# Forming three sums of input blocks from turned blocks alone, in the entries of a decoder block's three big products

## The chip, the cores and the metric

One core of one Trainium2 chip runs the whole kernel. The metric is the device time of one execution in microseconds (us), as the median of several runs.

## What is computed

A decoder block on 1024 tokens of width 1024 in float32: a SwiGLU half-step, a gated merge of two token mixers, a second half-step, a final norm. Cut to what matters here:

```python
h = x + 0.5 * swiglu(rms_norm(x, g1), w1, w3, w2)       # "f1"
proj = rms_norm(h, g2) @ w_in                           # "mix": q, k, v, pool input, gates
h = h + merged(proj) @ w_out
h = h + 0.5 * swiglu(rms_norm(h, g3), v1, v3, v2)       # "f2"
return rms_norm(h, g4)
```

Each of the three stages multiplies a normed input by wide weights: `rms_norm(h) @ w`.

## The kernel before

**Seven products.** The normed input is a matrix of 2 x 2 blocks: rows in two halves (token tiles 0 to 3, the lower, and 4 to 7, the upper; a tile is 128 tokens) and columns in two halves (LOWS, HIGHS, 512 each). As in Strassen's method in Winograd's form, a block product takes seven multiplications instead of eight. Their input sides are b11 and b21 (the lower tiles' two halves), b22 (the upper tiles' high half), and four sums: t1 = b12 - b11, t2 = b22 - t1, t3 = b22 - b12, t4 = t2 - b21, where b12 is the upper tiles' low half. All are held turned (features on the partitions), in two parts of a shorter format: `hi`, a rounded copy made by ScalarE, and `lo`, the remainder `source - hi`. A product is 12 matmuls of 128x512: weights hi by input hi, weights hi by input lo, weights lo by input hi.

**An entry.** `Entry.run` prepares the upper tiles while TensorE has products to do that need only b11 and b21. It occurs three times, in the stages f1, mix and f2. For each upper tile t: the norm scales the rows (`high(t, 1)`, VectorE, L282); TensorE turns b22 (`Rows`, four 128x128 transposes into one PSUM bank, L409), b12 (`turned`, four, L477) and the row difference HIGHS - LOWS, which POOL formed (L461; four transposes, L409). VectorE forms t1 in place of b12 (`first_less`, L471), t2 = turned difference + b11 (`second`, L465) and t4 in place of t2 (`fourth`, L468). The turned b11 and b21 of tile t - 4 are at hand in SBUF (`self.low`). `Parts` and `Rows` have ScalarE make the `hi` (L429, L411), and `lower` makes the `lo` on VectorE (L432, L416). Two products of TensorE stand in each turn of the loop, `product(i)` and `product(k)`; tile 7 has a passage of its own behind the loop, so that its first sums needed come first.

**Order.** The code runs under a manual schedule: each engine works through its instructions in the order in which the code issues them, and waits by semaphores for what another engine must have done. Two engines are kept from using one PSUM bank at a time: `second` therefore stands behind ScalarE's `hi` of the same bank. `self.more(n)` issues the operands of the first products behind the entry: the sum of weight blocks, ScalarE's rounding of it (L320, `wc`), and its remainder (L323, VectorE or POOL). The first of these products uses t2, then t3, t1 and t4 follow.

Of the kernel before, what the change touches and what calls it, by code (L numbers as in the profile page):

```python
# [10 lines left out]
F32 = mybir.dt.float32  # L11
F32R = mybir.dt.float32r
AF = mybir.ActivationFunctionType
OP = mybir.AluOpType
# [123 lines left out]
def tile_block(  # L138
# [29 lines left out]
    ve, ac, gp, pe = nc.vector, nc.scalar, nc.gpsimd, nc.tensor  # L168

    def sbuf(name, side="left", bufs=1):  # L170
        return tc.tile_pool(name=name, bufs=bufs, side=side, reuse_waits="tile")
# [7 lines left out]
    def bank(tag, name):  # L179
        return psum.tile([P, HALF], F32, tag=tag, name=name)  # L180
# [117 lines left out]
    LOWS, HIGHS = slice(0, HALF), slice(HALF, S)  # L298

    def sums_of_x(pool, name, order, **kw):  # L300
        return {
            s: tuple(pool.tile([P, 4, HALF], F32R, name=f"x{part}_{s}_{name}", **kw) for part in ("hi", "lo"))
            for s in order
        }
# [31 lines left out]
    class Quad:  # L336
# [49 lines left out]
        def run(self, m, back=True):  # L386
            if m not in self.w:
                self.operand(m)
            w, n = self.w.pop(m), self.n
            x = {1: "b11", 2: "b21", 3: "b22", 4: "t4", 5: "t1", 6: "t2", 7: "t3"}[m]  # L390
            key = {1: "x", 2: "x", 5: "v", 3: "v"}.get(m, m)
            first = key not in self.bank
            if first:
                self.bank[key] = bank("mm" if key in ("x", "v") else "acc", f"u_{self.sv.name}{n}{m}")
            self.sv.product(self.bank[key], w, x, start=first)
            if m == 3 and back:
                raws.back(2)
            return self.bank[key]

    class Rows:  # L400
# [14 lines left out]
        def lower(self):  # L415
            ve.tensor_tensor(self.lo, self.p, self.hi.bitcast(F32), op=OP.subtract)  # L416
# [5 lines left out]
    class Parts:  # L422
# [5 lines left out]
            self.src = src.rearrange("p (k q) -> p k q", k=4)  # L428
            ac.activation(self.hi, self.src, AF.Copy)  # L429

        def lower(self):
            ve.tensor_tensor(self.lo, self.src, self.hi.bitcast(F32), op=OP.subtract)  # L432

    class Entry:

# [17 lines left out]
        def run(self, high, after, first=0):  # L453


            X = self.sv.X

            def scaled_rows(t):
                y = high(t, 1)
                t3 = self.sv.half_tile("s", f"t3_{t}")  # L460
                gp.tensor_tensor(t3, y[:, HIGHS], y[:, LOWS], op=OP.subtract)  # L461
                return y, t3

            def second(r3, t2, t):
                ve.tensor_tensor(t2, r3.flat, self.low[t - 4][:, LOWS], op=OP.add)  # L465

            def fourth(t2, t):
                ve.tensor_tensor(t2, t2, self.low[t - 4][:, HIGHS], op=OP.subtract)  # L468

            def first_less(p12, t):  # L470
                ve.tensor_tensor(p12, p12, self.low[t - 4][:, LOWS], op=OP.subtract)  # L471

            def turned(y, t):
                p12 = bank("acc", f"x_b12_{t}")
                for j in range(4):
                    c = slice(j * P, (j + 1) * P)
                    pe.transpose(p12[:, c], y[:, c], ident)  # L477
                return p12

            y, t3 = scaled_rows(4)  # L480
            for t in range(4, NT - 1):
                i = first + 2 * (t - 4)
                k = i + 1
                self.product(i)
                self.operand(i + 2)
                high(t + 1, 0)
                s = Rows(X, "b22", y[:, HIGHS], t)
                self.out(i)
                p12 = turned(y, t)
                first_less(p12, t)  # L490
                r1 = Parts(X, "t1", p12, t)
                r3 = Rows(X, "t3", t3, t)
                t2 = bank("acc", f"x_t2_{t}")
                s.lower()
                r1.lower()
                self.product(k)
                y, t3 = scaled_rows(t + 1)
                self.operand(k + 2)
                second(r3, t2, t)
                r2 = Parts(X, "t2", t2, t)  # L500
                r3.lower()
                r2.lower()
                self.out(k)
                after(t)
                fourth(t2, t)
                if t < NT - 2:
                    r4 = Parts(X, "t4", t2, t)
                    if t > 4:
                        self.more(0, 1)
                    r4.lower()  # L510

            t = NT - 1
            i, k = i + 2, k + 2
            self.product(i)
            p3 = bank("acc", f"x_t3_{t}")
            p12 = turned(y, t)
            s = Rows(X, "b22", y[:, HIGHS], t, "mm")
            r3 = Rows(X, "t3", t3, t, p=p3)
            r4 = Parts(X, "t4", t2, t - 1)
            self.more(0, 2)  # L520
            t2 = bank("acc", f"x_t2_{t}")
            second(r3, t2, t)
            r4.lower()
            r2 = Parts(X, "t2", t2, t)
            r3.lower()
            self.more(0)
            r2.lower()
            self.product(k)
            self.out(i)
            first_less(p12, t)  # L530
            r1 = Parts(X, "t1", p12, t)
            self.more(1)
            r1.lower()
            fourth(t2, t)
            r4 = Parts(X, "t4", t2, t)
            s.lower()
            r4.lower()
            self.out(k)
            after(t)
# [366 lines left out]
    X = sums_of_x(scope.enter_context(sbuf("x1")), "f1", SUMS)  # L906
# [971 lines left out]
    def combine(hp, half, adds, lower):  # L1878

        c = (LOWS, HIGHS)[half]  # L1880
        o = [own[hp, g][:, c] for g in range(GROUPS)]
        for g in range(GROUPS):
            ve.tensor_tensor(o[g], o[g], factor_rows(hp, g, half), op=OP.mult)
            if g > 0:
                adds[g - 1].tensor_tensor(o[g], o[g], o[g - 1], op=OP.add)
            yield
        if half == 0:
            att_parts[hp] = [part_tile(f"att{hp}_{part}") for part in range(2)]
        hi, lo = (v[:, c] for v in att_parts[hp])
        ac.activation(hi, o[2], AF.Copy)  # L1890
        lower.tensor_tensor(lo, o[2], hi.bitcast(F32), op=OP.subtract)
        yield
# [114 lines left out]
    with tc.manual_schedule():  # L2007
# [3 lines left out]
        load_gate(1)  # L2011
        factors = [make_factors(hp, eng) for hp, eng in enumerate((gp, ve))]
        combines = [[combine(hp, half, adds, lower) for half in range(2)]
                    for hp, (adds, lower) in enumerate((((gp, gp), gp), ((gp, ve), ve)))]
        splits = {}
        for q in range(N // 2):
# [80 lines left out]
    op = wo.enter_context(sbuf("ops", "right"))  # L2097
# [390 lines left out]
```

## Time and profile before

| | |
|---|---|
| median of 3 runs | 1890.03 us (1889.73 to 1890.55) |
| span of the profiled execution | 1888.4 us |
| TensorE (PE) busy | 1878.1 us, 99% |
| VectorE (DVE) busy | 1345.8 us, 71% |
| ScalarE (ACT) busy | 773.1 us, 41% |
| POOL busy | 715.0 us, 38% |

The profiled execution is one run on the chip, and its times are those from which the terms below are taken. Its own time is not given apart from the span, which goes from its first to its last instruction. A row of the timeline reads: start in us from the start of the span, duration in us, engine, line of the kernel, operation, output<-input by the program's names (buffer numbers left out), shapes, the count of instructions merged into the row, and in brackets how long the engine sat idle before it and for whom. x_b is a PSUM bank with turned rows (b11, b12, b22), x_t one with a sum; xhi and xlo are the parts.

### The profile page before, as it was taken

What the parts mean: (1) busy time and instruction counts of PE and PEld (TensorE: products, weight loads), DVE (VectorE), ACT (ScalarE), POOL (GpSimd) and SP (SyncE); (2) the same over time, 40 slices, a digit from 0 to 9 for tenths busy, and PEclk for the clock granted to TensorE, in tenths of its full rate; (3) what the DMA queues carried; (4) which work ended last, traced back from release to release, by engine and by line L of the source; (5) the groups of instructions that cost most, each with busy time, mean ns of one, the idle gap of its engine ahead of it and who ended that gap; (6) DMA issues with size and microseconds to landing.
All of it is one profiled execution on the core that took longest, in us unless ns stands there. A gap on an engine that the chain in (4) does not pass through costs nothing.

```text
span 1888.4 us, 24712 instructions
## 1 busy us (share of the span) xinstructions
PE 1878.1 (99%) x8806; PEld 1559.8 (83%) x8806; DVE 1345.8 (71%) x1988; ACT 773.1 (41%) x1395; POOL 715.0 (38%) x536
## 2 busy tenths in 40 slices
PE   9999999999999999999999999999999999999998
PEld 8888888888888888888888888888888888888886
DVE  6877666558786776657885897887665566577867
ACT  7423333333344543334445772363233333334344
POOL 5433333331223354434555357543333333312221
PEclk9999999999999999999999999999999999999999
DMA  6154423336565526765578968644332223354654
GB/s 258 34 201 158 139 93 115 126 117 217 171 230 197 184 90 217 231 221 200 206 245 315 321 221 297 260 150 155 140 129 96 87 102 118 135 193 159 225 198 145
DMA packets 146035, 334.98 MB, mean 177 GB/s; under 512 B 17784, under 2 KB 39288, under 8 KB 144376
## 3 DMA queue, kind: packets, MB, share of 16 engines
q1 hardware_dynamic: 142168, 322.55, 49.4%
q10 hardware_dynamic: 3744, 10.85, 1.6%
q8 instruction: 69, 1.13, 0.2%
q14 instruction: 54, 0.44, 0.1%
HBM read 232.76 MB, written 100.60 MB: 177 GB/s over the span
## 4 chain that ended last, share of the span: by engine, by line
PE 54%; DVE 3%; ACT 2%; issue 1%; DMA 1%; POOL 0%; ACTq 0%; SPq 0%; DVEq 0%; POOLq 0%
PE u_mixm L332 15%; PE d_f L846 8%; PE wo L2168 4%; PE yp L1910 1%; PE u_f20b L332 1%; PE u_f21a L332 1%; PE u_f210b L332 1%; PE u_f210a L332 1%; PE u_f29b L332 1%; PE u_f29a L332 1%; PE u_f28b L332 1%; PE u_f28a L332 1%; PE u_f27b L332 1%; PE u_f27a L332 1%; PE u_f26b L332 1%; PE u_f25b L332 1%
## 5 line engine op out<-in xcount | busy, mean ns | idle before, releaser
L846 PE MATMUL d_f<-bhi_f,ahi_f 128*128 128x512 f32 x616 | 240.2, 390 | 0.0
L846 PE MATMUL d_f<-bhi_f,alo_f 128*128 128x512 f32 x616 | 239.7, 389 | 0.0
L846 PE MATMUL d_f<-blo_f,ahi_f 128*128 128x512 f32 x616 | 239.6, 389 | 0.0
L803 POOL TENSOR_TENSOR alo_f<-g_f,ahi_f 128x512 fp32r<-128x512 f32 x60 | 86.5, 1457 | 273.1 <-ACT ahi_f L799 273.1
L332 PE MATMUL u_mixm<-xhi_t_mix,wc_mixm 128*128 128x512 f32 x608 | 157.3, 391 | 0.2 <-ACT wc_mixm L320 0.2
L846 PEld LDWEIGHTS d_f<-bhi_f,ahi_f 128*128 128x128 f32 x616 | 115.6, 188 | 24.2 <-ACT h L420 0.4
L846 PEld LDWEIGHTS d_f<-bhi_f,alo_f 128*128 128x128 f32 x616 | 115.6, 188 | 24.1
L846 PEld LDWEIGHTS d_f<-blo_f,ahi_f 128*128 128x128 f32 x616 | 115.6, 188 | 23.9
L332 PEld LDWEIGHTS u_mixm<-xhi_t_mix,wc_mixm 128*128 128x128 f32 x608 | 113.5, 188 | 24.0 <-ACT wc_mixm L320 0.7
L332 PE MATMUL u_mixm<-xhi_b_mix,wc_mixm 128*128 128x512 f32 x456 | 120.3, 391 | 0.0
L323 POOL TENSOR_TENSOR wc_mixm<-s_mixm,wc_mixm 128x512 fp32r<-128x512 f32 x52 | 76.8, 1477 | 107.1 <-ACT wc_mixm L320 94.2
L332 PEld LDWEIGHTS u_mixm<-xhi_b_mix,wc_mixm 128*128 128x128 f32 x456 | 84.9, 188 | 17.3
L320 ACT ACTIVATE wc_mixm<-s_mixm 128x512 fp32r<-128x512 f32 x76 | 47.0, 628 | 111.8 <-DVE s_mixm L374 56.0
L799 ACT ACTIVATE ahi_f<-g_f 128x1024 fp32r<-128x1024 f32 x84 | 81.9, 975 | 4.9 <-DMA g_f<-gs_f 4.9
L332 PE MATMUL u_mixm<-xlo_t_mix,wc_mixm 128*128 128x512 f32 x304 | 81.3, 389 | 0.0
L323 POOL TENSOR_TENSOR wc_mixm<-raw,wc_mixm 128x512 fp32r<-128x512 f32 x40 | 60.2, 1505 | 40.2 <-ACT wc_mixm L320 29.5
L2168 PE MATMUL wo<-w_o,o_hi 128*128 128x512 f32 x224 | 69.4, 391 | 0.0
L799 ACT ACTIVATE bhi_f<-s_f2w 128x512 fp32r<-128x512 f32 x55 | 32.9, 628 | 86.3 <-DVE s_f2w L821 67.3
L799 ACT ACTIVATE bhi_f<-s_f1w 128x512 fp32r<-128x512 f32 x55 | 33.0, 629 | 83.6 <-DVE s_f1w L821 70.3
L332 PEld LDWEIGHTS u_mixm<-xlo_t_mix,wc_mixm 128*128 128x128 f32 x304 | 57.1, 188 | 12.0
L803 DVE TENSOR_TENSOR alo_f<-g_f,ahi_f 128x1024 fp32r<-128x1024 f32 (+1 forms) x48 | 57.6, 1200 | 9.4 <-ACT ahi_f L799 9.4
L332 PE MATMUL u_mixm<-xlo_b_mix,wc_mixm 128*128 128x512 f32 x228 | 61.0, 389 | 0.0
(1351 smaller groups left out, 4765.5 us busy)
## 6 DMA issues: line engine op xcount, KB each, us to landing
g_f<-gs_f SPq DMA_DIRECT2D x70, 512.0 KB
gs_f<-y_f SPq DMA_DIRECT2D x88, 256.0 KB
raw<-in_w2a_dram SPq DMA_DIRECT2D x35, 512.0 KB
raw<-in_w2b_dram SPq DMA_DIRECT2D x35, 512.0 KB
gs_f<-gb_f SPq DMA_DIRECT2D x46, 256.0 KB
raw<-in_w1a_dram SPq DMA_DIRECT2D x22, 512.0 KB
raw<-in_w3a_dram SPq DMA_DIRECT2D x22, 512.0 KB
raw<-in_w1b_dram SPq DMA_DIRECT2D x22, 512.0 KB
```

The source lines that it names most:

```text
L320: ac.activation(w[:, 0], src, AF.Copy)
L323: eng.tensor_tensor(w[:, 1], src, w[:, 0].bitcast(F32), op=OP.subtract)
L332: pe.matmul(p, a, b, start=(start and n == 0), stop=(n == 11), skip_group_check=not start)
L799: ac.activation(hi[:, c], src, AF.Copy)
L803: eng.tensor_tensor(lo[:, d], src[:, o], hi[:, d].bitcast(F32), op=OP.subtract)
L846: pe.matmul(self.banks[m][t], l, r, start=(first and q == 0), stop=(last and q == 2))
L1910: pe.matmul(p, a, b, start=(j == 0), stop=(j == 11))
L2168: pe.matmul(banks[m][t], l, r, start=(st == 0 and j == 0 and q == 0), stop=(st == 1 and j == 1 and q == 2))
```

## The change

The row difference, its POOL instruction and its four transposes are gone, so an upper tile takes eight transposes. t1 is written to an SBUF tile and no longer in place of b12, so the bank with b12 stays; t2 is formed as turned b22 - t1 (`second`), and t3 as t2 - b11 (`third`, written over the bank with b12). In tiles 4 to 6 the remainder of t1 is made by POOL instead of VectorE. `first_less` of tile 7 stands ahead of `second`, no longer near the end.

```diff
-        def lower(self):
-            ve.tensor_tensor(self.lo, self.src, self.hi.bitcast(F32), op=OP.subtract)
+        def lower(self, eng=ve):
+            eng.tensor_tensor(self.lo, self.src, self.hi.bitcast(F32), op=OP.subtract)
...
             def scaled_rows(t):
-                y = high(t, 1)
-                t3 = self.sv.half_tile("s", f"t3_{t}")
-                gp.tensor_tensor(t3, y[:, HIGHS], y[:, LOWS], op=OP.subtract)
-                return y, t3
-
-            def second(r3, t2, t):
-                ve.tensor_tensor(t2, r3.flat, self.low[t - 4][:, LOWS], op=OP.add)
+                return high(t, 1)
+
+            def first_less(p12, t):
+                t1 = self.sv.half_tile("s", f"t1_{t}")
+                ve.tensor_tensor(t1, p12, self.low[t - 4][:, LOWS], op=OP.subtract)
+                return t1
+
+            def second(s, t1, t2):
+                ve.tensor_tensor(t2, s.flat, t1, op=OP.subtract)
+
+            def third(t2, p, t):
+                ve.tensor_tensor(p, t2, self.low[t - 4][:, LOWS], op=OP.subtract)
...
-            def first_less(p12, t):
-                ve.tensor_tensor(p12, p12, self.low[t - 4][:, LOWS], op=OP.subtract)
...
                 p12 = turned(y, t)
-                first_less(p12, t)
-                r1 = Parts(X, "t1", p12, t)
-                r3 = Rows(X, "t3", t3, t)
+                t1 = first_less(p12, t)
+                r1 = Parts(X, "t1", t1, t)
                 t2 = bank("acc", f"x_t2_{t}")
                 s.lower()
-                r1.lower()
+                second(s, t1, t2)
+                r1.lower(gp)
                 self.product(k)
-                y, t3 = scaled_rows(t + 1)
+                y = scaled_rows(t + 1)
                 self.operand(k + 2)
-                second(r3, t2, t)
                 r2 = Parts(X, "t2", t2, t)
+                third(t2, p12, t)
+                r3 = Parts(X, "t3", p12, t)
+                r2.lower()
                 r3.lower()
-                r2.lower()
                 self.out(k)
...
             self.product(i)
-            p3 = bank("acc", f"x_t3_{t}")
             p12 = turned(y, t)
             s = Rows(X, "b22", y[:, HIGHS], t, "mm")
-            r3 = Rows(X, "t3", t3, t, p=p3)
+            t1 = first_less(p12, t)
             r4 = Parts(X, "t4", t2, t - 1)
             self.more(0, 2)
             t2 = bank("acc", f"x_t2_{t}")
-            second(r3, t2, t)
+            second(s, t1, t2)
             r4.lower()
             r2 = Parts(X, "t2", t2, t)
-            r3.lower()
+            third(t2, p12, t)
+            r3 = Parts(X, "t3", p12, t)
             self.more(0)
             r2.lower()
+            r3.lower()
             self.product(k)
             self.out(i)
-            first_less(p12, t)
-            r1 = Parts(X, "t1", p12, t)
+            r1 = Parts(X, "t1", t1, t)
             self.more(1)
             r1.lower()
```

How this moves instructions in the queues, at two places. VectorE, tile 5 of the mixing entry, before and after (L370 is a weight sum; in the changed kernel first_less is L463, second L467, third L470, fourth L473, and s_mixt1 is t1 in SBUF):

```order
L471 TENSOR_TENSOR x_b12_5_5631<-x_b12_5_5631,h1_3197 128x512
L416 TENSOR_TENSOR xlo_b22_mix_5524<-x_b22_5_5624,xhi_b22_mix_5523 128x4x128
L432 TENSOR_TENSOR xlo_t1_mix_5528<-x_b12_5_5631,xhi_t1_mix_5527 128x4x128
L282 SCALAR_TENSOR_TENSOR hn_mix6_5496<-h6_3207,nst_6_5497,gain_mix_3211 128x1024
L465 TENSOR_TENSOR x_t2_5_5644<-x_t3_5_5638,h1_3197 128x512
L416 TENSOR_TENSOR xlo_t3_mix_5526<-x_t3_5_5638,xhi_t3_mix_5525 128x4x128
L432 TENSOR_TENSOR xlo_t2_mix_5519<-x_t2_5_5644,xhi_t2_mix_5518 128x4x128
L468 TENSOR_TENSOR x_t2_5_5644<-x_t2_5_5644,h1_3197 128x512
```

The same place in the changed kernel:

```order
L463 TENSOR_TENSOR s_mixt1_5_5609<-x_b12_5_5604,h1_3177 128x512
L416 TENSOR_TENSOR xlo_b22_mix_5504<-x_b22_5_5597,xhi_b22_mix_5503 128x4x128
L467 TENSOR_TENSOR x_t2_5_5612<-x_b22_5_5597,s_mixt1_5_5609 128x512
L282 SCALAR_TENSOR_TENSOR hn_mix6_5476<-h6_3187,nst_6_5477,gain_mix_3191 128x1024
L470 TENSOR_TENSOR x_b12_5_5604<-x_t2_5_5612,h1_3177 128x512
L432 TENSOR_TENSOR xlo_t2_mix_5499<-x_t2_5_5612,xhi_t2_mix_5498 128x4x128
L432 TENSOR_TENSOR xlo_t3_mix_5506<-x_b12_5_5604,xhi_t3_mix_5505 128x4x128
L473 TENSOR_TENSOR x_t2_5_5612<-x_t2_5_5612,h1_3177 128x512
```

Eight instructions stand in both; t2 is formed ahead of the next tile's scaling (L282) instead of behind it, the remainder of t1 has left the queue, and t3's formation has come in.

ScalarE, tile 7 of the last entry, up to the rounding of the first weights behind it (wc), before:

```order
L411 ACTIVATE xhi_b22_f2_11388<-x_b22_7_11617 128x4x128
L411 ACTIVATE xhi_t3_f2_11382<-x_t3_7_11611 128x4x128
L429 ACTIVATE xhi_t4_f2_11386<-x_t2_6_11570 128x4x128
L429 ACTIVATE xhi_t2_f2_11380<-x_t2_7_11631 128x4x128
L320 ACTIVATE wc_f20a6_11636<-s_f20a2_11629 128x512
```

And after:

```order
L411 ACTIVATE xhi_b22_f2_11348<-x_b22_7_11559 128x4x128
L429 ACTIVATE xhi_t4_f2_11346<-x_t2_6_11513 128x4x128
L429 ACTIVATE xhi_t2_f2_11340<-x_t2_7_11570 128x4x128
L429 ACTIVATE xhi_t3_f2_11342<-x_b12_7_11554 128x4x128
L320 ACTIVATE wc_f20a6_11576<-s_f20a2_11568 128x512
```

The rounding of t3 has moved from ahead of t2's to behind it, directly ahead of the weights'. VectorE's queue there, before:

```order
L468 TENSOR_TENSOR x_t2_6_11570<-x_t2_6_11570,h2_again_10578 128x512
L465 TENSOR_TENSOR x_t2_7_11631<-x_t3_7_11611,h3_again_10592 128x512
L432 TENSOR_TENSOR xlo_t4_f2_11387<-x_t2_6_11570,xhi_t4_f2_11386 128x4x128
L416 TENSOR_TENSOR xlo_t3_f2_11383<-x_t3_7_11611,xhi_t3_f2_11382 128x4x128
L323 TENSOR_TENSOR wc_f20a6_11636<-s_f20a2_11629,wc_f20a6_11636 128x512
L432 TENSOR_TENSOR xlo_t2_f2_11381<-x_t2_7_11631,xhi_t2_f2_11380 128x4x128
L471 TENSOR_TENSOR x_b12_7_11612<-x_b12_7_11612,h3_again_10592 128x512
```

And after:

```order
L473 TENSOR_TENSOR x_t2_6_11513<-x_t2_6_11513,h2_again_10538 128x512
L463 TENSOR_TENSOR s_f2t1_7_11565<-x_b12_7_11554,h3_again_10552 128x512
L467 TENSOR_TENSOR x_t2_7_11570<-x_b22_7_11559,s_f2t1_7_11565 128x512
L432 TENSOR_TENSOR xlo_t4_f2_11347<-x_t2_6_11513,xhi_t4_f2_11346 128x4x128
L470 TENSOR_TENSOR x_b12_7_11554<-x_t2_7_11570,h3_again_10552 128x512
L323 TENSOR_TENSOR wc_f20a6_11576<-s_f20a2_11568,wc_f20a6_11576 128x512
L432 TENSOR_TENSOR xlo_t2_f2_11341<-x_t2_7_11570,xhi_t2_f2_11340 128x4x128
L432 TENSOR_TENSOR xlo_t3_f2_11343<-x_b12_7_11554,xhi_t3_f2_11342 128x4x128
```

t1 of tile 7 has moved from behind the remainders to directly behind L473, t2 is formed from it, and t3 stands between the remainders of t4 and of the weights.

More of the change, by code (lines that the diff above doesn't have):

```diff
@@ L478, in turned @@
                 return p12
-            y, t3 = scaled_rows(4)
+            y = scaled_rows(4)
             for t in range(4, NT - 1):
```

## The prediction, made before the changed kernel was run

> **What bounds the kernel now.** I read the page first, then TensorE's own waits, then busy time by stretch.
>
> ```profile
> span 1888.4 us, 24712 instructions
> PE 1878.1 (99%) x8806; PEld 1559.8 (83%) x8806; DVE 1345.8 (71%) x1988; ACT 773.1 (41%) x1395; POOL 715.0 (38%) x536
> ...
> PE x_t L409 <- POOL s_f1t L461: 0.8, 1, 0.8
> ...
> 30.00:61.00 31.00, 30.18 (x158) 25.32 (x158) 26.59 (x40) 22.84 (x46) 20.38 (x18) 1.00 0.20 69
> 640.00:690.00 50.00, 50.00 (x245) 41.76 (x244) 39.09 (x59) 27.55 (x51) 23.88 (x21) 1.00 0.31 103
> 1240.00:1285.00 45.00, 44.87 (x221) 37.04 (x220) 36.92 (x59) 25.40 (x48) 23.89 (x20) 1.00 0.33 117
> ```
>
> TensorE is busy 99% of the span, so a transpose taken away shortens the run if, and only if, nothing else becomes late. The third row says TensorE waited once in an entry, 0.8 us for the row difference. The last three are the stretches of the three entries (columns: length, then busy PE, PEld, DVE, ACT, POOL). VectorE's 71% over the span is 86%, 78% and 82% there: the entries are where it could become the bound, and the average hides that.
>
> **Work removed from TensorE.** Tiles 4 and 5 of the first entry, TensorE alone:
>
> ```profile
> 38.25 0.65 PE L409 MATMUL x_t<-ident,s_f1t 128*128 128x128 f32 x4 [0.82 <-POOL s_f1t L461]
> ...
> 41.51 1.07 PE L332 MATMUL u_f11a<-xhi_b_f,wc_f11a 128*128 128x512 f32 x4
> ...
> 44.24 0.60 PE L409 MATMUL x_b<-ident,x 128*128 128x128 f32 x4
> 44.67 0.60 PE L477 MATMUL x_b<-ident,x 128*128 128x128 f32 x4
> 45.11 0.60 PE L409 MATMUL x_t<-ident,s_f1t 128*128 128x128 f32 x4
> ```
>
> Four transposes advance TensorE by 45.11 - 44.67 = 0.44 us. Twelve groups go (four tiles, three entries): 5.2 us, 1.74 per entry. In the first entry the 0.82 us wait at 38.25 goes with them: 2.56 there. Together 6.0 us (0.32%) is all that there is to win.
>
> **VectorE inside a tile.** Tile 5 of the mixing entry, before:
>
> ```profile
> 661.94 0.69 DVE L432 TENSOR_TENSOR xlo_t_mix<-x_t,xhi_t_mix 128x512 fp32r<-128x512 f32 x1 [0.66 <-ACT xhi_t_mix L429]
> ...
> 662.61 0.69 DVE L471 TENSOR_TENSOR x_b<-x_b,h 128x512 f32<-128x512 f32 x1
> 663.21 0.68 DVE L416 TENSOR_TENSOR xlo_b_mix<-x_b,xhi_b_mix 128x512 fp32r<-128x512 f32 x1
> 663.97 0.69 DVE L432 TENSOR_TENSOR xlo_t_mix<-x_b,xhi_t_mix 128x512 fp32r<-128x512 f32 x1
> 664.57 1.27 DVE L282 SCALAR_TENSOR_TENSOR hn_mix<-h,nst,gain_mix 128x1024 f32<-128x1024 f32 x1
> 665.77 0.69 DVE L465 TENSOR_TENSOR x_t<-x_t,h 128x512 f32<-128x512 f32 x1
> 666.37 0.68 DVE L416 TENSOR_TENSOR xlo_t_mix<-x_t,xhi_t_mix 128x512 fp32r<-128x512 f32 x1
> 667.13 0.69 DVE L432 TENSOR_TENSOR xlo_t_mix<-x_t,xhi_t_mix 128x512 fp32r<-128x512 f32 x1
> 667.85 0.70 DVE L468 TENSOR_TENSOR x_t<-x_t,h 128x512 f32<-128x512 f32 x1
> ...
> 669.88 0.69 DVE L471 TENSOR_TENSOR x_b<-x_b,h 128x512 f32<-128x512 f32 x1
> ```
>
> An operation of 0.69 lets the next start after 0.60; one that needs a ScalarE rounding just made starts after 0.76 (663.21 to 663.97), one that needs the previous VectorE result after 0.72 (667.13 to 667.85). From tile 5 to tile 6 (662.61 to 669.88) VectorE takes 7.3 us, while TensorE's tile is 6.8 long: two products of 2.73 (41.51 to 44.24) and three groups of 0.44. So VectorE is the slower of the two in the loop; TensorE doesn't wait only because its transposes are ahead of what VectorE does with them.
>
> The count on VectorE stays: the difference's addition (L465) becomes `second`, L468 stays, `third` is added, and `r1.lower` goes to POOL, which gives up the row difference in exchange (both 128x512 from SBUF; L461 takes 1.27, below, so POOL's load is about even). What changes is the waits: `r1.lower`'s 0.16 goes, since `second` needs only VectorE's t1, with `s.lower` between; `r3.lower` now waits about as long for its rounding as `r2.lower` did; L468 no longer overwrites what was read just before it, 0.12 less where no output stands between them (tiles 5 and 6 of the mixing entry, tile 6 of the others; in tile 4 ScalarE's square stands before the rounding for which 661.94 waited). VectorE reaches L468 of tile 6 earlier by 3 x 0.16 + 2 x 0.12 = 0.72 in the mixing entry and 0.60 in the last. The first entry gains 0.40 more:
>
> ```profile
> 36.92 1.27 POOL L461 TENSOR_TENSOR s_f1t<-x 128x512 f32<-128x512 f32 x1
> ...
> 39.40 0.56 POOL L279 TENSOR_TENSOR nst<-nst,mhalf 128x1 f32<-128x1 f32 x1
> ...
> 39.99 1.28 DVE L282 SCALAR_TENSOR_TENSOR x<-x,nst,gain_ffn 128x1024 f32<-128x1024 f32 x1 [0.40 <-POOL nst L279]
> ```
>
> Without L461 the power is done some 1.2 earlier (the length of L461) and VectorE's 0.40 wait is gone: 1.00 in all.
>
> **The end of an entry: the step that decides.** The first product after an entry needs t2 of all tiles and its weights' rounding (L320). Last entry, then L468 of tile 6 and that product's start in the other two:
>
> ```profile
> 1270.82 0.70 DVE L468 TENSOR_TENSOR x_t<-x_t,h_again 128x512 f32<-128x512 f32 x1
> ...
> 1271.50 0.59 ACT L411 ACTIVATE xhi_t_f<-x_t 128x512 fp32r<-128x512 f32 x1
> 1272.12 0.70 DVE L465 TENSOR_TENSOR x_t<-x_t,h_again 128x512 f32<-128x512 f32 x1 [0.60 <-ACT xhi_t_f L411]
> ...
> 1272.86 0.60 ACT L429 ACTIVATE xhi_t_f<-x_t 128x512 fp32r<-128x512 f32 x1 [0.28 <-DVE x_t L465]
> ...
> 1273.35 0.62 ACT L320 ACTIVATE wc_f20a<-s_f20a 128x512 fp32r<-128x512 f32 x1
> ...
> 1274.03 1.19 PE L332 MATMUL u_f20a<-xhi_t_f,wc_f20a 128*128 128x512 f32 x4
> ...
> 1275.35 1.21 PE L332 MATMUL u_f20a<-xlo_t_f,wc_f20a 128*128 128x512 f32 x4
> ...
> 58.77 0.70 DVE L468 TENSOR_TENSOR x_t<-x_t,x 128x512 f32<-128x512 f32 x1
> ...
> 61.93 0.50 PE L332 MATMUL u_f10a<-xhi_t_f,wc_f10a 128*128 128x512 f32 x1
> ...
> 675.12 0.70 DVE L468 TENSOR_TENSOR x_t<-x_t,h 128x512 f32<-128x512 f32 x1
> ...
> 678.76 0.50 PE L332 MATMUL u_mixm<-xhi_t_mix,wc_mixm 128*128 128x512 f32 x1
> ```
>
> Before, L468 to product took 3.16, 3.64 and 3.21 us, and TensorE came there just in time. After, between them stand: t1 (0.60 behind L468), `second` (0.72, it needs t1), t2's rounding on ScalarE (0.74, as 1272.12 to 1272.86), `third` (0.62, as 1271.50 to 1272.12: it reads the bank that ScalarE rounds from, as L465 did), t3's rounding (0.74), the weights' rounding, queued behind t3's on ScalarE (0.49, as 1272.86 to 1273.35), the product (0.68, as 1273.35 to 1274.03): 4.59. That is longer by 1.43, 0.95 and 1.38; less the credits 1.00, 0.72 and 0.60, the product starts later by 0.43, 0.23 and 0.78 than now. TensorE, 2.56 or 1.74 early, stands still for some 3.0, 2.0 and 2.5 us and the whole saving is lost. In the last entry TensorE also waits 0.3 at 1275.35 for t2's low part; VectorE's low part of the weights still stands before it, so that stays.
>
> **Sum:** 0.43 + 0.23 + 0.78 = +1.4 us. The rest I cost at nothing: first-part and low-part work behind the product (`r1.lower`, L473, `s.lower`, `r4.lower`) has the next products, 2.73 each, to hide in; if not, it shows as a second wait of under 0.7 per entry. Three PSUM banks a tile instead of four make no transpose wait. No DMA moves; the gain load in ScalarE's queue stays between t2's and t3's rounding and waits for a VectorE result that `third` also stands behind. The credits are the least sure. If none came, the sum would be +3.8 (1.43 + 0.95 + 1.38); if every 0.16 wait of a tile went, three per tile, it would be at most 3 x 3 x 0.16 + 0.24 = 1.7 per entry, and 0.40 in the first: -1.7. I take +1.4, by the one wait per tile that the order takes away. The profiled span is 1888.4; the runs' median 1890.03 lies 1.6 above it, taken as unchanged: **1891.4 us**.
>
> **Rivals.** (a) *The saving arrives whole:* 1890.0 - 6.0 = 1884.0. Needs VectorE 2 us or more ahead at L468; nothing in its rows gives that. (b) *Nothing net:* VectorE is earlier by more waits than the order takes away, since ScalarE has less queued ahead of its roundings: 1888.4 (the bound of -1.7) to 1890.5. (c) *The gaps drop TensorE's clock,* slower. At the end of the run:
>
> ```profile
> 1881.02 0.39 PE L846 MATMUL d_f<-bhi_f,alo_f 128*128 128x512 f32 x1
> ...
> 1883.00:1884.00 1.00, 0.00 (x0) 0.00 (x0) 0.19 (x2) 0.73 (x3) 0.55 (x1) 0.70 0.74 277
> 1884.00:1885.00 1.00, 0.00 (x0) 0.00 (x0) 0.72 (x1) 0.72 (x1) 0.00 (x0) 0.50 0.94 346
> ```
>
> A mean clock of 0.70 in the second after 1883 means a fall to 0.5 at 1883.4, 2.0 us after the last matmul ended at 1881.4; the new gaps are 2.0 to 3.0 us. A product of 2.73 at half clock costs 2.7 more, so one drop gives 1894.1, three 1899.5. It decides from the first gap whose place makes the clock fall; against it, the gaps may be split by an earlier short wait for an operand. The Trainium skill ("TensorE: Matmul & The Clock Gate", Part 1) lets the gate close only after an idle window of about 3.4 us; by that rule no gap here is long enough and this rival falls away. The end of this trace differs with 2.0 us, and the measurement decides; by the page's time to warm up, also 3.4 us, an estimate for one drop would be +1.7 instead of +2.7.
>
> **Numbers.** Forecast (a late product, no clock drop) 0.64; nothing net 0.14; a clock drop 0.16; the whole saving 0.06. About 0.2% (3.8 us) is what a measurement tells from no change: forecast and "nothing net" lie within it, a drop beyond (1893.8). So faster 0.06, same 0.78, slower 0.16. The range goes from 1888.4, the lower bound of the sum, to 1894.5, which takes in no credits (1893.8) and one drop (1894.1); it leaves out the whole saving and more than one drop, about 0.14.
>
> **What would show it.** Right: TensorE's waits name ScalarE's weight rounding at the first product of each entry, 2 to 3 us each; busy PE is down by about 5; `third` starts just behind ScalarE's t2 rounding; transposes of tile 7 come early and the product after them no earlier than now. Wrong: these gaps are under 1 us (VectorE was faster than its pitch), or the granted clock falls below 1.00 after them, or later stages have new waits, which nothing here foresees.

## The result and the profile after

The changed kernel takes 1901.25 us (median of 5 runs, 1900.24 to 1901.49); the kernel before took 1890.46 us in 5 runs beside it. The ratio is 1.0055, 95% interval 1.0043 to 1.0067: 10.8 us slower, outside the forecast range of 1888.4 to 1894.5. The profiled span is 1899.5 us, 11.1 above that of before.

From the page of the changed kernel, then TensorE's own waits (total, times, longest), then the busy time in the stretch of the first entry (length, then PE, PEld, DVE, ACT, POOL, clock):

```profile
span 1899.5 us, 24604 instructions
PE 1876.6 (99%) x8758; PEld 1554.9 (82%) x8758; DVE 1356.7 (71%) x1991; ACT 774.4 (41%) x1395; POOL 720.4 (38%) x533
```
```profile
PE u_mixm L332 <- ACT wc_mixm L320: 2.4, 2, 1.7
PE u_f20a L332 <- ACT wc_f20a L320: 1.7, 1, 1.7
PE u_f10a L332 <- ACT wc_f10a L320: 1.7, 1, 1.7
PE u_mixm L332 <- ACT y_m L1231: 1.6, 2, 0.9
PE u_f12a L332 <- ACT y_f L586: 1.5, 1, 1.5
```
```profile
30.00:61.00 31.00, 27.92 (x136) 22.38 (x136) 27.43 (x38) 22.06 (x43) 21.84 (x17) 1.00 0.20 64
```

The 48 transposes are gone (8758 matmuls for 8806). In 30 to 61 us TensorE is busy for 27.9 us; before, it was for 30.2. VectorE's busy time over the span rises by 10.9 us, though it got only three instructions more: some of its instructions have become longer. The view of one source line says which. The row scaling L282, minimum, median and maximum in ns, first of the changed kernel, then of before:

```profile
L282 DVE SCALAR_TENSOR_TENSOR x<-x,nst,gain_ffn x4: 2009/2238/2308, 33.3 to 56.5; 128x1024 f32<-128x1024 f32 x4
L282 DVE SCALAR_TENSOR_TENSOR hn_mix<-h,nst,gain_mix x4: 1285/2117/2250, 653.0 to 676.8; 128x1024 f32<-128x1024 f32 x4
L282 DVE SCALAR_TENSOR_TENSOR hn_f<-h_again,nst,gain_ffn x4: 1275/2024/2227, 1252.4 to 1276.0; 128x1024 f32<-128x1024 f32 x4
```
```profile
L282 DVE SCALAR_TENSOR_TENSOR x<-x,nst,gain_ffn x4: 1277/1280/2314, 33.1 to 55.5; 128x1024 f32<-128x1024 f32 x4
L282 DVE SCALAR_TENSOR_TENSOR hn_mix<-h,nst,gain_mix x4: 1274/1276/1285, 649.1 to 671.8; 128x1024 f32<-128x1024 f32 x4
L282 DVE SCALAR_TENSOR_TENSOR hn_f<-h_again,nst,gain_ffn x4: 1275/1275/1276, 1245.0 to 1267.5; 128x1024 f32<-128x1024 f32 x4
```

The same instruction on the same shapes takes 2.0 to 2.25 us in the three loop turns of each entry instead of 1.28; the nine together are 7.7 us longer (2.65 + 2.64 + 2.44, from their rows). (The 2308 and 2314 ns of the first group are the scaling of tile 4, ahead of the loop; it is long in both kernels.) What lies beside it is in the timeline of the first entry, VectorE and POOL, changed kernel; the last two rows are the same place of the kernel before:

```profile
39.17 1.29 POOL L432 TENSOR_TENSOR xlo_t_f<-s_f1t,xhi_t_f 128x512 fp32r<-128x512 f32 x1 [0.21 <-ACT xhi_t_f L429]
39.53 2.01 DVE L282 SCALAR_TENSOR_TENSOR x<-x,nst,gain_ffn 128x1024 f32<-128x1024 f32 x1
40.42 2.28 POOL L323 TENSOR_TENSOR wc_f11b<-raw,wc_f11b 128x512 fp32r<-128x512 f32 x1
...
47.78 1.29 POOL L432 TENSOR_TENSOR xlo_t_f<-s_f1t,xhi_t_f 128x512 fp32r<-128x512 f32 x1
47.90 2.25 DVE L282 SCALAR_TENSOR_TENSOR x<-x,nst,gain_ffn 128x1024 f32<-128x1024 f32 x1
49.03 2.26 POOL L323 TENSOR_TENSOR wc_f12b<-raw,wc_f12b 128x512 fp32r<-128x512 f32 x1
```
```profile
41.35 1.29 POOL L461 TENSOR_TENSOR s_f1t<-x 128x512 f32<-128x512 f32 x1 [1.40 <-DVE x L282]
42.61 1.29 POOL L323 TENSOR_TENSOR wc_f11b<-raw,wc_f11b 128x512 fp32r<-128x512 f32 x1
```

Read the ends. POOL's first operation ends at 39.17 + 1.29 = 40.46, the scaling at 41.54, 1.08 later. In the next tile 49.07 and 50.15: again 1.08. The same distance after overlaps of different length fits a scaling that stands until POOL's operation is done, not one that runs slowly. POOL's next operation in turn ends 1.16 behind the scaling (42.70), 1.14 in the next tile (51.29), which is why L323 shows 2.28 instead of 1.29. By these rows each waits for the whole of the other. Before, none of this could happen in the loop: the row difference waited for the scaled rows (1.40 us, row L461), and it kept L323 behind it. That wait was what kept POOL still while VectorE scaled.

The Trainium skill ("SBUF — State Buffer", section "Who interferes with whom") says that a VectorE instruction with two SBUF inputs contends with a GpSimd (POOL) instruction that reads SBUF, and that contention for the port pair they share is "an exclusive lock". These rows agree, with 1.08 and 1.16 us from the end of the one to the end of the other.

How long each entry took, from the start of tile 4's scaling to the start of the first product behind the entry (timeline rows; the kernels with numbers are the experiments below):

| | f1 | mix | f2 | sum against before |
|---|---|---|---|---|
| before | 28.87 | 29.63 | 29.08 | |
| changed | 32.02 | 32.63 | 32.35 | +9.4 |
| 3: before, one more POOL operation | 31.02 | 30.32 | 29.75 | +3.5 |
| 6: changed, POOL held | 29.33 | 30.26 | 29.90 | +1.9 |
| 7: and weights ahead of t3 | 27.97 | 28.90 | 28.56 | -2.2 |
| 9: and t1, t2 early, t4 later | 27.47 | 28.39 | 28.04 | -3.7 |

Of the 10.8 us, 9.4 are lost inside the three entries.

### The profile page after: what moved, and what is told of

Its sections match the earlier page's. It is cut to its first block, busy times and chain, and to the rows that moved or that the text cites. A ratio compares the mean times of both kernels' runs of the same rounds, so it can differ in the third digit from the quotient of the medians.

```text
span 1899.5 us, 24604 instructions
## 1 busy us (share of the span) xinstructions
PE 1876.6 (99%) x8758; PEld 1554.9 (82%) x8758; DVE 1356.7 (71%) x1991; ACT 774.4 (41%) x1395; POOL 720.4 (38%) x533
## 3 DMA queue, kind: packets, MB, share of 16 engines
q8 instruction: 69, 1.13, 0.2%
## 4 chain that ended last, share of the span: by engine, by line
PE 53%; DVE 4%; ACT 2%; issue 1%; DMA 1%; POOL 1%; ACTq 0%; SPq 0%; DVEq 0%; POOLq 0%
PE u_mixm L332 15%; PE d_f L849 8%; PE wo L2171 4%; PE yp L1913 1%; PE u_f24a L332 1%; PE u_f210b L332 1%; PE u_f210a L332 1%; PE u_f29b L332 1%; PE u_f29a L332 1%; PE u_f28b L332 1%; PE u_f28a L332 1%; PE u_f27b L332 1%; PE u_f27a L332 1%; PE u_f26b L332 1%; PE u_f26a L332 1%
## 5 line engine op out<-in xcount | busy, mean ns | idle before, releaser
L332 PE MATMUL u_mixm<-xhi_t_mix,wc_mixm 128*128 128x512 f32 x608 | 157.4, 391 | 2.4 <-ACT wc_mixm L320 2.4
L332 PEld LDWEIGHTS u_mixm<-xhi_t_mix,wc_mixm 128*128 128x128 f32 x608 | 113.5, 188 | 26.3 <-ACT wc_mixm L320 3.1
L332 PE MATMUL u_mixm<-xhi_b_mix,wc_mixm 128*128 128x512 f32 x456 | 120.6, 392 | 1.6 <-ACT y_m L1231 1.6
L323 POOL TENSOR_TENSOR wc_mixm<-s_mixm,wc_mixm 128x512 fp32r<-128x512 f32 x52 | 76.8, 1478 | 107.8 <-ACT wc_mixm L320 97.5
L332 PEld LDWEIGHTS u_mixm<-xhi_b_mix,wc_mixm 128*128 128x128 f32 x456 | 84.9, 188 | 19.4 <-ACT y_m L1231 2.3
L332 PE MATMUL u_mixm<-xlo_t_mix,wc_mixm 128*128 128x512 f32 x304 | 81.4, 389 | 0.0
L323 POOL TENSOR_TENSOR wc_mixm<-raw,wc_mixm 128x512 fp32r<-128x512 f32 x40 | 63.0, 1578 | 42.8 <-ACT wc_mixm L320 37.6
L332 PEld LDWEIGHTS u_mixm<-xlo_t_mix,wc_mixm 128*128 128x128 f32 x304 | 57.1, 188 | 12.0
L332 PE MATMUL u_mixm<-xlo_b_mix,wc_mixm 128*128 128x512 f32 x228 | 61.0, 390 | 0.0
```

Source lines behind the costliest of these rows:

```text
L323: eng.tensor_tensor(w[:, 1], src, w[:, 0].bitcast(F32), op=OP.subtract)
L332: pe.matmul(p, a, b, start=(start and n == 0), stop=(n == 11), skip_group_check=not start)
```

## The experiments

The theory: POOL's operations beside the scaling stretch it. Rivals: `r1.lower` is itself late on POOL and waited for; or the chain at the entry's end is longer than forecast, whatever POOL does.

**1. The remainder of t1 back on VectorE.**

```diff
-                r1.lower(gp)
+                r1.lower()
```

> The changed kernel, with the remainder of t1 (r1.lower) back on VectorE, all else as changed. POOL then has one SBUF operation beside the row scaling (L282), the rounding remainder of the next operand (L323), instead of two. Theory (VectorE's scaling, which reads two SBUF tiles, and any SBUF operation of POOL stretch each other): the scaling is still stretched, to about 1.9 to 2.1 us, because L323 still lies beside it; TensorE waits at the entries' ends still; 1896 to 1900 us. Rival 1 (r1.lower is slow on POOL and is itself what is waited for): the cause is gone, 1891.9 us (before plus the 1.4 that was forecast for the chain). Rival 2 (the chain at an entry's end is longer than forecast, whatever POOL does): 1900 to 1902.

Measured 1907.02 us, ratio 1.0089 (1.0075 to 1.0103), slower still. First entry, tile 4, and one of TensorE's waits:

```profile
39.22 0.68 DVE L432 TENSOR_TENSOR xlo_t_f<-s_f1t,xhi_t_f 128x512 fp32r<-128x512 f32 x1
...
39.37 1.68 POOL L323 TENSOR_TENSOR wc_f11b<-raw,wc_f11b 128x512 fp32r<-128x512 f32 x1 [0.69 <-ACT wc_f11b L320]
...
39.81 2.32 DVE L282 SCALAR_TENSOR_TENSOR x<-x,nst,gain_ffn 128x1024 f32<-128x1024 f32 x1
```
```profile
PE x_b L409 <- DVE x L282: 1.8, 1, 1.8
```

L323 alone does it: it ends at 41.05, the scaling at 42.13, 1.08 later. TensorE waits 1.8 us for one such scaling. All nine scalings took 2.30 to 2.32, so it is not `r1.lower` on POOL that is slow, and rival 1 falls. The expectation of 1896 to 1900 was too low by its own reckoning: it left out that VectorE gets nine operations back, 9 x 0.60 = 5.4 us, and that the stretch is then 9 x 1.03 = 9.3. Added to the kernel with POOL held (experiment 6, 1892.9) that makes 1907.6; this sum was made after the result.

**2. POOL held behind the scaling.** A POOL addition of one column reads the scaled rows; what follows in POOL's queue waits with it, as it did for the row difference.

```diff
-                r1.lower(gp)
                 self.product(k)
                 y = scaled_rows(t + 1)
+                held = small.tile([P, 1], F32, tag="held", name=f"held_{t}")
+                gp.tensor_tensor(held, y[:, 0:1], mhalf, op=OP.add)
+                r1.lower(gp)
                 self.operand(k + 2)
```

> The changed kernel, with r1.lower and the next operand's remainder on POOL both put behind an addition on POOL of one column that reads the scaled rows, so that POOL does nothing beside the scaling, as it was in the kernel before, where the row difference waited for them. Same work on POOL otherwise. Theory (contention): L282 back to 1.28 us in all tiles, first product of the entries 2 to 3 us earlier than in the changed kernel, 1891 to 1893 us (before plus the forecast 1.4). Rival 1 (r1.lower on POOL is late): r1.lower comes later here than in the changed kernel, so no gain, 1901 us or more. Rival 2 (chain longer than forecast): 1900 to 1902, with L282 at 1.28.

Measured 1911.57 us, ratio 1.0115 (1.0100 to 1.0131): a miss by 19 us, though L282 was back at 1.28 in all nine places. Its page says where the time is:

```profile
PE 1893.4 (99%) x8758; PEld 1556.2 (81%) x8758; DVE 1347.7 (71%) x1991; ACT 774.6 (41%) x1395; POOL 709.5 (37%) x542
```

TensorE is *busy* 16.8 us longer than in the changed kernel with the same matmuls. In the stages f1 and mix the products (L332) had medians of 392 to 395 ns where they had 389, between the entries as much as in them; in f2 they stayed at 389. The held column's tile lies in SBUF ahead of the products' operands. Experiments 5 and 6 test that.

**3. The kernel before with one more POOL operation beside the scaling,** in each loop turn, overwritten by the true row difference and read by nobody.

```diff
+                t3 = self.sv.half_tile("s", f"t3_{t}")
                 y = high(t, 1)
-                t3 = self.sv.half_tile("s", f"t3_{t}")
+                if t > 4:
+                    gp.tensor_tensor(t3, self.low[t - 4][:, HIGHS], self.low[t - 4][:, LOWS], op=OP.subtract)
                 gp.tensor_tensor(t3, y[:, HIGHS], y[:, LOWS], op=OP.subtract)
```

> The kernel before, with one more POOL operation per loop tile (128x512 difference of two SBUF halves, overwritten by the true row difference) that runs beside the scaling; 9 in all, none read by anyone. Theory (contention): L282 goes from 1.28 to 2.0 to 2.3 us in tiles 5 to 7 of all entries, VectorE comes later by 0.75 to 1 us per tile, and of that 2 to 3 us per entry less the slack that TensorE has before: 1893 to 1899 us. Rivals 1 and 2: L282 stays at 1.28 and the time at 1890.5.

Measured 1893.85 us, ratio 1.0020 (1.0011 to 1.0029): 3.7 us slower, at the lower end of what the theory said; both rivals said no change.

```profile
39.89 2.30 DVE L282 SCALAR_TENSOR_TENSOR x<-x,nst,gain_ffn 128x1024 f32<-128x1024 f32 x1 [0.39 <-POOL nst L279]
...
39.81 1.30 POOL L462 TENSOR_TENSOR s_f1t<-x 128x512 f32<-128x512 f32 x1
```

The extra operation (L462) ends at 41.11, the scaling at 42.19: 1.08 again. Seven of the nine scalings were stretched, 5.3 us in all, and the entries grew by 3.5; the rest was hidden. Beside the other two the extra operation had ended before the scaling began. An operation whose result nothing waits for costs time here, only by where it lies.

**4. POOL held, and the weights' rounding ahead of t3's in tile 7.** The edit of experiment 2, and:

```diff
-            r3 = Parts(X, "t3", p12, t)
             self.more(0)
+            r3 = Parts(X, "t3", p12, t)
             r2.lower()
```

> As the one before the last (POOL kept idle beside the scaling), and in tile 7 the rounding of the next product's weights (L320) is put ahead of the rounding of t3 on ScalarE, so that the product waits for t2 and its weights, not for t3. By the forecast's own terms the chain from L468's place to the product is shorter by third's wait and t3's rounding, 0.62 + 0.74 = 1.36 us: 4.59 goes to 3.23, about what it was before. If the chain is what remains (theory: contention plus the forecast chain), the time is 1891.9 less some 1.0 to 1.36 per entry: 1888 to 1889 us, faster than before by 0.1%. Rival (the chain isn't what TensorE waits for): the same as with POOL held alone.

Measured 1907.78 us, ratio 1.0093 (1.0079 to 1.0107). It misses for the same reason as experiment 2, and is 3.8 us faster than that one.

**5. The kernel before, operands moved by 128 bytes.** No instruction differs.

```diff
-    consts.tile([P, 32], F32, name="pad2")
+    consts.tile([P, 64], F32, name="pad2")
```

> The kernel before with its second padding tile 64 columns wide instead of 32: no instruction added or moved, but the operands of the L332 products (the rounded parts of the seven sums) begin 128 bytes further into each partition of SBUF, as they did in the two kernels with POOL held. New theory (the one-column tile shifted those operands, and that made each L332 matmul some 4 to 6 ns longer, 17 us of busy TensorE): median of an L332 matmul 393 ns instead of 389, 1905 to 1908 us. Rival (the longer matmuls came from POOL's moved work): 1890 us, 389 ns.

Measured 1909.22 us, ratio 1.0101 (1.0087 to 1.0114): 18.8 us slower by padding alone. One group of mix products before and with the shift (min/median/max in ns), then, all with the shift, one group of f2 products, one of the down products (L846) and the page's busy time:

```profile
L332 PE MATMUL u_mixm<-xhi_b_mix,wc_mixm x456: 388/389/481, 651.5 to 1030.4; 128*128 128x512 f32 x152
```
```profile
L332 PE MATMUL u_mixm<-xhi_b_mix,wc_mixm x456: 387/395/483, 663.0 to 1050.8; 128*128 128x512 f32 x152
```
```profile
L332 PE MATMUL u_f24a<-xhi_t_f,wc_f24a x32: 389/389/390, 1428.6 to 1442.0; 128*128 128x512 f32 x32
```
```profile
L846 PE MATMUL d_f<-blo_f,ahi_f x616: 387/389/398, 449.1 to 1901.5; 128*128 128x512 f32 x154
```
```profile
PE 1899.2 (99%) x8806; PEld 1561.5 (82%) x8806; DVE 1348.8 (71%) x1988; ACT 773.6 (41%) x1395; POOL 712.4 (37%) x536
```

389 becomes 393 to 396 in the groups of f1 and mix; the products of f2 stay at 389 or 390 and the down products at 389; busy TensorE rises by 21.1 us. The tile addresses of the built kernels say what sets them apart. In f1 and mix the padding moves the inputs' parts (xhi, xlo) by 128 bytes and leaves the weights (wc) where they were; in f2, and for the down products, both operands move together. So the inputs' new place alone doesn't cost the time, since they moved as far in f2; what differs is where a product's two operands lie to each other. Other distances weren't run. So experiments 2 and 4 measured an address beside what they meant to measure. Their like with the padding tile left out, which puts the operands back where they were, are 6 and 7.

**6. POOL held, operands at their old place.** As 2, without `pad2`.

> POOL held behind the scaling as in the second experiment, with the second padding tile left out so that the operands of the products lie where they lay before. Theory (POOL beside the scaling cost the changed kernel its time, and the addresses spoilt the second experiment): L332 median 389 ns, L282 1.28 us, 1911.6 less 16.8 = 1894.8 us by the busy time, between 1892 and 1895; clearly under the changed kernel's 1901.3. Rival (the entries' end chain is what costs): 1900 to 1902.

Measured 1892.92 us, ratio 1.0013 (1.0004 to 1.0022). The scaling and POOL in tile 4 of the first entry (lines are one lower here), and TensorE's waits:

```profile
39.27 1.27 DVE L281 SCALAR_TENSOR_TENSOR x<-x,nst,gain_ffn 128x1024 f32<-128x1024 f32 x1
...
40.62 0.19 POOL L499 TENSOR_TENSOR held<-x,mhalf 128x1 f32<-128x1 f32 x1 [1.89 <-DVE x L281]
40.76 1.30 POOL L431 TENSOR_TENSOR xlo_t_f<-s_f1t,xhi_t_f 128x512 fp32r<-128x512 f32 x1
42.02 1.29 POOL L322 TENSOR_TENSOR wc_f11b<-raw,wc_f11b 128x512 fp32r<-128x512 f32 x1
```
```profile
PE u_mixm L331 <- ACT wc_mixm L319: 2.0, 2, 1.7
...
PE u_f10a L331 <- ACT wc_f10a L319: 1.7, 1, 1.7
PE u_f20a L331 <- ACT wc_f20a L319: 1.7, 1, 1.7
...
PE u_f12a L331 <- ACT y_f L587: 0.7, 1, 0.7
```

All lengths are normal again. 8.3 of the 10.8 us are gone, with the same work on the same engines, one tiny instruction per loop turn added and `r1.lower` *later* than in the changed kernel. The nine scalings are 7.7 us shorter and the entries 7.5. Rival 2, which had 1900 to 1902 here, falls as the main cause; it keeps the remaining 2.5.

**7. POOL held, weights' rounding ahead of t3's, old place.** As 4, without `pad2`.

> The same, with the weights' rounding ahead of t3's in tile 7, at the old addresses. Theory: the first product of an entry waits under 0.5 us instead of 1.7 us; the kernel with POOL held less 3 x 1.2 = 3.6, so 1888 to 1891.5 us. Rival (the chain isn't what TensorE waits for): the same time as the kernel with POOL held alone.

Measured 1889.09 us, ratio 0.9993 (0.9984 to 1.0002), 3.8 under experiment 6. The first products now wait 0.33 to 0.37 us. So the chain through t3's rounding was what TensorE waited for once the contention was out of the way.

**8. t1 and t2 of tile 7 ahead of the subtraction for t4 of tile 6,** whose rounding goes behind the weights'. Against experiment 7:

```diff
-                fourth(t2, t)
                 if t < NT - 2:
+                    fourth(t2, t)
...
             t1 = first_less(p12, t)
-            r4 = Parts(X, "t4", t2, t - 1)
             self.more(0, 2)
-            t2 = bank("acc", f"x_t2_{t}")
+            t2, t4 = bank("acc", f"x_t2_{t}"), t2
             second(s, t1, t2)
-            r4.lower()
             r2 = Parts(X, "t2", t2, t)
+            fourth(t4, t - 1)
             third(t2, p12, t)
             self.more(0)
             r3 = Parts(X, "t3", p12, t)
+            r4 = Parts(X, "t4", t4, t - 1)
             r2.lower()
             r3.lower()
+            r4.lower()
```

> As the one before, and t1 and t2 of tile 7 are formed on VectorE ahead of the subtraction for t4 of tile 6 (L473 of the changed kernel), 0.60 us of work, whose rounding goes behind the weights'. Theory (the end chain is still the bound by some 0.3 to 0.6 us per entry): 0.9 to 1.8 us less than the one before, 1887 to 1890 us, with no wait left at the first product. Rival (TensorE is no longer late there): no change.

Measured 1888.89 us, ratio 0.9991 (0.9982 to 1.0000): 0.2 under experiment 7 where 0.9 to 1.8 had been expected, no gain to be told. The wait at the first product is gone, and stands at the second one instead (0.40 us for the rounding of its weights, whose sum on VectorE now comes behind t4's remainder). Moved, not removed.

**9. And t4's remainder behind that sum.** Against experiment 8:

```diff
             r3.lower()
-            r4.lower()
             self.product(k)
...
             self.more(1)
+            r4.lower()
             r1.lower()
```

> As the kernel with t1 and t2 of tile 7 formed early, and t4's low part of tile 6 goes behind the second product's weight sum on VectorE, 0.60 us earlier for that sum. Theory (what is left at an entry's end is the 0.40 us by which the second product waits for its weights): up to 0.4 x 3 = 1.2 us less, 1887.7 to 1889 us. Rival: the wait moves on once more and the time stays at 1888.9.

Measured 1887.08 us, ratio 0.9983 (0.9974 to 0.9991): 3.3 us faster than the kernel before, the version that beats both; it is 1.8 under experiment 8, more than the 1.2 at most that was expected. The first two products behind the first entry, which start without a wait:

```profile
60.29 1.20 PE L331 MATMUL u_f10a<-xhi_t_f,wc_f10a 128*128 128x512 f32 x4
61.32 1.07 PE L331 MATMUL u_f10a<-xlo_t_f,wc_f10a 128*128 128x512 f32 x4
62.23 2.05 PE L331 MATMUL u_f10a<-xhi_t_f,wc_f10a 128*128 128x512 f32 x8
```

Of the 6.0 us that the removed transposes and the one wait could give, 3.7 arrive in the entries.

**10. The changed kernel with nothing but the weights ahead of t3.** The second part of experiment 4's edit alone.

> The changed kernel as it is, with POOL beside the scaling, and only the weights' rounding ahead of t3's in tile 7. Theory (two causes that add up, contention of some 8 us and a chain of t2, t3 and weights): 1901.3 less 3 x 1.2 = 3.6, 1897 to 1899 us, L282 still at 2.0 to 2.3 us. Rival (with the scaling stretched, something else is late there, so the chain gives nothing): 1901.

Measured 1896.56 us, ratio 1.0031 (1.0019 to 1.0043): 4.7 less than the changed kernel, somewhat more than the 2.3 to 4.3 expected, while the scalings stay stretched:

```profile
L282 DVE SCALAR_TENSOR_TENSOR hn_mix<-h,nst,gain_mix x4: 1285/2116/2244, 651.6 to 675.4; 128x1024 f32<-128x1024 f32 x4
```

So there are two causes, and either can be taken away alone: the contention (8.3 us, changed against 6; 7.5, experiment 10 against 7) and the order at the end (4.7 or 3.8).

## Why the prediction was wrong, step by step

**The step that failed** is the one sentence on POOL: "`r1.lower` goes to POOL, which gives up the row difference in exchange (both 128x512 from SBUF ..., so POOL's load is about even)". The load is even; the place is not. The row difference read the scaled rows, so it could not lie beside the scaling, and it held L323 behind it. `r1.lower` needs no scaled rows, starts as the scaling starts, and lets L323 follow at once. Costed at nothing, it cost 7.5 us in the entries and 8.3 in the whole. The trace of before had it: L282's maximum of 2314 ns in the f1 group above is the scaling of tile 4, which ends at 35.37, 1.09 behind a POOL operation beside it (L323, 32.91 to 34.28). The prediction took 1.28 for all.

**The chain at the end of an entry** was right. Forecast from the last subtraction (L468, now L473) to the product: 4.59 us. The rows of the changed kernel in the first entry, VectorE, ScalarE and TensorE:

```profile
60.67 0.69 DVE L473 TENSOR_TENSOR x_t<-x_t,x 128x512 f32<-128x512 f32 x1
61.27 0.68 DVE L463 TENSOR_TENSOR s_f1t<-x_b,x 128x512 f32<-128x512 f32 x1
62.05 0.70 DVE L467 TENSOR_TENSOR x_t<-x_b,s_f1t 128x512 f32<-128x512 f32 x1
...
62.79 0.60 ACT L429 ACTIVATE xhi_t_f<-x_t 128x512 fp32r<-128x512 f32 x1 [0.80 <-DVE x_t L467]
...
63.42 0.70 DVE L470 TENSOR_TENSOR x_b<-x_t,x 128x512 f32<-128x512 f32 x1
...
64.15 0.60 ACT L429 ACTIVATE xhi_t_f<-x_b 128x512 fp32r<-128x512 f32 x1 [0.77 <-DVE x_b L470]
64.64 0.62 ACT L320 ACTIVATE wc_f10a<-s_f10a 128x512 fp32r<-128x512 f32 x1
...
65.32 1.20 PE L332 MATMUL u_f10a<-xhi_t_f,wc_f10a 128*128 128x512 f32 x4 [1.72 <-ACT wc_f10a L320]
```

65.32 - 60.67 = 4.65, and the same within 0.01 in the other two entries; the links are the forecast ones within 0.06: `second` 0.78 behind t1 (forecast 0.72), `third` 0.63 behind t2's rounding, t3's rounding 0.73 later, the weights 0.49, the product 0.68.

**VectorE's credits inside the loop** (1.00, 0.72, 0.60) show in experiment 6, where the scaling has its old length: L468's place comes earlier by 1.02, 0.37 and 0.61. The mixing entry's was half of what was forecast.

**The sum,** +0.43 + 0.23 + 0.78 = +1.4, measured there at +0.46, +0.63, +0.82 = +1.9, and 1892.92 us for a forecast of 1891.4. With POOL held, the forecast range would have held the time.

**TensorE's gaps** were forecast at 3.0, 2.0 and 2.5 us, all of it at the first product, and named rightly (ScalarE's weight rounding); they are 1.72 to 1.73 in all three entries, because TensorE had already lost time earlier in the same entries. In the first it waited 1.5 us at u_f12a and 0.7 at u_f12b for ScalarE to copy an older product out of the bank (L586 above, L614). The first of these copies starts 2.2 us behind VectorE's subtraction for t4 in all three kernels (54.90 - 52.69, 52.93 - 50.71 in experiment 6, 53.72 - 51.50 before), so a late VectorE makes it late too. This is not the contention alone: with POOL held (experiment 6) the gaps are 1.7 as well, and u_f12a still waits 0.7. A TensorE that is early by its transposes meets VectorE's pace inside the entry already; the prediction had put all of the standing still at its end.

**Busy TensorE** was to fall by about 5; it fell by 1.5, and by 4.3 in experiment 6. What the page counts as busy in the changed kernel beyond that isn't settled.

**The rivals.** The whole saving (1884.0) did not come, and nothing net (1888.4 to 1890.5) is excluded. The clock drop did not occur: the granted clock is 1.00 in the entry's stretch and from 61 to 66 us, where the first gap lies. The gaps of 1.7 us are shorter than the 2.0 of the trace of before and than the 3.4 of the Trainium skill ("TensorE: Matmul & The Clock Gate", Part 1), so no run here tells which of the two would have held. The 2.0 is no fixed length: worked out in the same way, the clock fell 2.6 us after the last matmul in the changed kernel, 3.2 in experiment 6 and 4.4 in experiment 2. "Slower" came by a mechanism that was not among the rivals, and its chance of 0.16 belonged to another cause.

**No DMA moves, no transpose waits for a bank:** in TensorE's waits of the changed kernel the transposes of the entries name only the scaling (0.7 us at most, the contention's own). The products do wait for a bank, as just told; the prediction had looked at the transposes alone.

## What to carry to other kernels

When an operation is moved to another engine, don't ask only how long it takes and how full that engine is, but what kept it (and the queue behind it) from running at the moment where it will now run: a data dependence that is taken away may have been the only thing that kept POOL off VectorE's operations on two SBUF tiles. Look at the maximum beside the median in the view of a source line, and at its neighbour in time, before you cost an overlap at nothing. And when an experiment adds a tile, keep every other tile where it was, or measure the shift by itself.

## What was not expected of the hardware

- A VectorE operation on two SBUF tiles (128x1024, 1.28 us alone) ended 1.07 to 1.09 us after the end of the POOL operation beside it in the entries of the changed kernel and of experiments 1 and 3, and a POOL one (128x512, 1.29 alone) ended 1.13 to 1.16 after VectorE's in the changed kernel; VectorE operations with one input from PSUM beside POOL kept their 0.67 to 0.70. The longest of the nine in experiment 1 was 2.32 us.
- 128 bytes of padding that moved one operand of the products and not the other raised the median matmul from 389 ns to 393 to 396 and the kernel by 18.8 us, at a granted clock of 0.999 over the run; products of which both operands moved stayed at 389 or 390. Why the distance matters, and at which distances, stays open.
